# A two-layer hybrid decoder with the residual kept token-major, and 512-column matmuls throughout

## The chip, the cores and the metric

The kernel runs on one core of a Trainium2 chip. TensorE (PE) multiplies: it loads a stationary operand of 128x128 and streams a moving operand of up to 512 columns past it, and adds the products up in PSUM. VectorE (DVE) and ScalarE (ACT) do elementwise work, GpSimd (POOL) a little of it, and SyncE (SP) issues most of the loads. The metric is device time in microseconds for one execution, as the median of several runs. Lower is better.

## The reference

The input x is 256 tokens of 2048 features, in float32. Each of two layers adds a mixer and then a dense MLP to the residual, each behind an RMS norm:

```python
for i in range(DEPTH):                       # DEPTH = 2
    hn = rms_norm(h, mixer_norm[i])
    mix = diff_attention(hn, ...) if i == 0 else mamba2_mixer(hn, ...)
    h = h + mix
    h = h + jnp.square(jax.nn.relu(rms_norm(h, mlp_norm[i]) @ w1[i])) @ w2[i]
```

`diff_attention` has 8 heads. For each, two query and two key vectors of 128 are normed and rotated, two causal softmax maps are subtracted, and the result multiplies values of width 256; the heads are normed and projected by w_o. `mamba2_mixer` projects to gates z, channels x, B, C and 64 time steps dt, runs a causal convolution of 4 taps, a chunked scan over two chunks of 128 tokens, a gate and a group norm, and projects from 4096 to 2048 features by w_out. The MLP goes from 2048 to 8192 and back.

## The kernel before

Everything is held feature-major: a tile has 128 features on the partitions and the 256 tokens along the free dimension. The residual is eight tiles `h[j]` of [128, 2, 256], 256 features each.

All weights are float32 and come in pieces of [128, 1024], 512 KB, by `load` (SP's queue, six buffers `raw`). `split_weights` splits each piece exactly into two float32r parts: ACT rounds to `wh`, DVE subtracts to get `wl` (L138, L139, four buffers each). Activations are split in the same way; an entry of `acts` is [128, 2, 256], the high part beside the low part. A product is then made of three terms: high weight times high activation, high times low, and low times high.

`sub_block` multiplies one piece, 128 output features over 8 k-tiles of 128. It has two forms. Where the accumulator has room for one sum (*narrow*), each k-tile takes three matmuls of 256 columns, L151, L152 and L158, 24 for a piece. Where it has room for two (*wide*), high and low activations are streamed together, 512 columns, into two sums (L149), and L158 adds the low weights: 16 matmuls for a piece. The two sums are added afterwards on ACT and DVE.

- narrow: `pair` (queries, keys, Mamba's in-projection `win`), `block` (`wdt`), `half_pair` (the output projections `wo` and `wout`, eight k-tiles at a time, each result added to `h` by L280);
- wide: `wide_pair` (both MLP matrices; w1's sums are joined by L479 and L480, w2's added to `h` by L284);
- `token_pair` (values): activations are stationary and 256 weight columns stream (L211), 24 matmuls for a piece. The result has tokens on the partitions.

The order of the work is written out by hand. `Side` holds two queues of generators (norms, attention inside a head, convolution, scan); `side.tick()` is called three times for each piece and issues the next step of each queue between the matmuls. So the small matmuls of these steps, into PSUM tiles `aux`, lie among the projections.

The norms: `norm_input(j)` squares `h[j]` on ACT (L235), adds the squares up on POOL (L236), and makes the next stage's activations, `h[j] * gain` split in two, by L243 on ACT and L244 on DVE. `norm_stats` adds up over the partitions with a matrix of ones (L126) and computes 1/rms as a tile `rstd` that is the same on all partitions; it is multiplied in behind the projection (L481 in the MLP, L705 and L584 in Mamba). At the start x is loaded in eight tiles, between the first weights. The last stage stores `h[j]` by SP's queue as each is done.

Of the kernel before, what the change touches and what calls it, by code (L numbers as in the profile page):

```python
# [36 lines left out]
# columns of the packed parameters  # L37
# [51 lines left out]
def trunk_kernel(ctx: ExitStack, tc: tile.TileContext, x, par, rope, qk, wv, wo, w10, w20, win, wdt, wout, w11, w21, out):  # L89
# [27 lines left out]

    def split(src, t):
        """float32 [P, n] -> the two float32r parts that add up to it, t [P, 2, n]."""
        S.copy(out=t[:, 0, :], in_=src)  # L120
        V.tensor_tensor(out=t[:, 1, :], in0=src, in1=t[:, 0, :].bitcast(F32), op=ALU.subtract)

    def sums(out, t):
        """The sums over the partitions of what was split, on every partition."""
        for i in range(2):
            PE.matmul(out, lhsT=ones_r, rhs=t[:, i, :], start=(i == 0), stop=(i == 1))  # L126

    side = Side()
    h = [const.tile([P, 2, T], F32, name=f"h{j}") for j in range(KT // 2)]
    sqacc = const.tile([P, 2, T], F32, name="sqacc")  # L130

# [10 lines left out]
    def sub_block(w, acts, acc, start, stop):  # L142
        """128 output features over 8 k-tiles. acc has room for a sum [P, T], or for two [P, 2, T] that add up to it."""
        wh, wl = w
        wide = len(acc.shape) == 3
        for k, act in enumerate(acts):
            wk = wh[:, k * P:(k + 1) * P]
            if wide:
                PE.matmul(acc, lhsT=wk, rhs=act, start=(start and k == 0), stop=False)  # L149
            else:  # L150
                PE.matmul(acc, lhsT=wk, rhs=act[:, 0, :], start=(start and k == 0), stop=False)  # L151
                PE.matmul(acc, lhsT=wk, rhs=act[:, 1, :], start=False, stop=False)  # L152
            if k % 4 == 3:
                side.tick()
        if wide:
            acc = acc[:, 0, :]
        for k, act in enumerate(acts):
            PE.matmul(acc, lhsT=wl[:, k * P:(k + 1) * P], rhs=act[:, 0, :], start=False, stop=(stop and k == 7))  # L158
        side.tick()

    def load(src, s, n=1):
        """A piece of the weights, [128, 1024]."""
        raw = wp.tile([P, 1024], F32, tag="raw", bufs=6, name="raw")
        w = 1024 // n
        for i in range(n):
            nc.sync.dma_start(out=raw[:, i * w:(i + 1) * w], in_=src[s, :, i * w:(i + 1) * w])
        return raw

    def block(src, acts, acc):
        """128 output features over 16 k-tiles."""  # L170
        raw = [load(src, s) for s in range(2)]
        for s in range(2):
            sub_block(split_weights(raw[s]), acts[8 * s:8 * s + 8], acc, s == 0, s == 1)
# [4 lines left out]
    def pair(src, b, acts):  # L178
        """Two blocks."""
        pp = bank()  # L180
        for t in range(2):
            block(src[b + t], acts, pp[:, t, :])
        return pp

    def wide_pair(src, b, acts):
        """Two blocks, each as two sums."""
        pp = [bank() for _ in range(2)]
        for s in range(2):
            raw = [load(src[b + t], s) for t in range(2)]
            for t in range(2):  # L190
                sub_block(split_weights(raw[t]), acts[8 * s:8 * s + 8], pp[t], s == 0, s == 1)
        return pp

    def half_pair(src, acts):
        """Two blocks of 128 output features over 8 k-tiles."""
        pp = bank()
        raw = [load(src, t) for t in range(2)]
        for t in range(2):
            sub_block(split_weights(raw[t]), acts, pp[:, t, :], True, True)
        return pp  # L200

    def token_pair(src, acts):
        """256 output features over 16 k-tiles, tokens on the partitions."""
        pp = [bank() for _ in range(2)]
        for s in range(4):
            wh, wl = split_weights(load(src, s))
            for first, w in ((True, wh), (False, wl)):
                for k in range(4):
                    for t in range(2):
                        for i in range(2 if first else 1):  # L210
                            PE.matmul(pp[t][:, 0, :], lhsT=acts[4 * s + k][:, i, t * P:(t + 1) * P], rhs=w[:, k * T:(k + 1) * T],  # L211
                                      start=(first and s + k + i == 0), stop=(not first and s + k == 6))
                    if k == 3 or (first and k == 1):
# [7 lines left out]
    def split_pair(src):  # L221
        """float32 [P, 2, T] in SBUF -> its float32r parts."""
# [6 lines left out]
    def norm_square(j):  # L229
        """The sum of the squares of h[j]."""  # L230
        if j == 0:
            S.activation(sqacc, h[j], AF.Square)
        else:
            sq = const.tile([P, 2, T], F32, tag="nsq", bufs=1, name="nsq")
            S.activation(sq, h[j], AF.Square)  # L235
            G.tensor_tensor(out=sqacc, in0=sqacc, in1=sq, op=ALU.add)  # L236

    def norm_gain(j, gain):
        """h[j] * gain, whose 1/rms comes after the projection."""
        t, parts = act_pair()  # L240
        for i in range(2):
            g = pa[:, gain + 2 * j + i:gain + 2 * j + i + 1]
            S.activation(t[:, i, 0, :], h[j][:, i, :], AF.Identity, scale=g)  # L243
            V.scalar_tensor_tensor(out=t[:, i, 1, :], in0=h[j][:, i, :], scalar=g, in1=t[:, i, 0, :].bitcast(F32),  # L244
# [3 lines left out]
    def norm_input(j, gain):  # L248
        norm_square(j)
        return norm_gain(j, gain)  # L250

    def rsqrt(pool, t, n, tag, bufs=1):
        """t ** -0.5 by exp(-ln(t) / 2) and one Newton step."""
# [9 lines left out]
    mean = const.tile([P, T], F32, name="mean")  # L263
    rstd = const.tile([P, T], F32, name="rstd")

    def norm_stats():
        V.tensor_tensor(out=mean, in0=sqacc[:, 0, :], in1=sqacc[:, 1, :], op=ALU.add)
        parts = const.tile([P, 2, T], F32R, tag="nsq", bufs=1, name="nss")
        split(mean, parts)
        yield from wait(5)  # L270
        ss = aux()
        sums(ss[:, 0:T], parts)
        yield
        V.tensor_scalar(out=mean, in0=ss[:, 0:T], scalar1=1.0 / D, scalar2=EPS, op0=ALU.mult, op1=ALU.add)
        c = rsqrt(const, mean, T, "n")
        V.tensor_copy(out=rstd, in_=c)
        yield

    def residual(pp, j):
        V.tensor_tensor(out=h[j], in0=pp, in1=h[j], op=ALU.add)  # L280

    def residual_wide(pp, dst):
        for i in (1, 0):
            V.tensor_tensor(out=dst, in0=pp[:, i, :], in1=dst, op=ALU.add)  # L284
# [6 lines left out]
    for j in range(KT // 2):  # L291
        nc.sync.dma_start(out=h[j], in_=x[j])
        if j in (0, 3, 5):
            raw.append(load(qk[len(raw) % 2], len(raw) // 2, 1 if j else 2))
    raw.append(load(qk[1], 1))
    for s in range(2):
        for j in range(4 * s, 4 * s + 4):
            xs += norm_gain(j, C_MIX0)
            if j == 4 * s:
                w = split_weights(raw[2 * s], 1 if s else 2)  # L300
        for t in range(2):
            sub_block(w if t == 0 else split_weights(raw[2 * s + 1]), xs[8 * s:8 * s + 8], first[t][:, 0, :], s == 0, s == 1)
    for j in range(KT // 2):
        norm_square(j)

    with tc.tile_pool(name="att", bufs=1) as ap:
# [18 lines left out]
        def setup():  # L325
            yield from wait(2)
            yield from norm_stats()
            V.tensor_scalar_mul(epsm, mean, EPS)
            yield

        def setup_v():
            yield from wait(20)
            rt = aux()
            for t in range(2):
                PE.matmul(rt[:, t:t + 1], lhsT=rstd[:, t * P:(t + 1) * P], rhs=ident[:, 0:1], start=True, stop=True)
            V.tensor_copy(out=rtok, in_=rt[:, 0:2])
            yield
# [108 lines left out]
        for hd in range(NH):  # L446
            qkn = ap.tile([P, 4, T], F32, tag="qkn", bufs=2, name="qkn")
            pq = qkn[:, 0:2, :]
            if hd:
                pq = pair(qk, 4 * hd, xs)  # L450
            else:
                for t in range(2):
                    S.copy(out=pq[:, t, :], in_=first[t][:, 0, :])
# [379 lines left out]
```

## Time and profile before

| | |
|---|---|
| median of 3 runs | 2554.76 us (2554.24 to 2554.98) |
| span of the profiled execution, first to last instruction | 2551.7 us |
| the same execution's time with what lies around the span | not recorded; the median is 3.06 us above the span |
| busy: PE, PEld, DVE, ACT, POOL | 100%, 92%, 67%, 52%, 2% |
| granted TensorE clock | 1.000 |
| HBM read, written | 464.78 MB, 2.16 MB |

PE is the stream of matmuls and PEld the loads of stationary operands, which overlap it. In a row of a group, the first number behind the bar is the busy time in us (overlaps counted once), the next the mean of one instruction in ns, then the engine's idle time just before the group and what ended it. In the chain of work a row is a start, a duration and what ran; consecutive matmuls there take the time by which each moved the chain on, so it shows their pitch and not their latency. A row of stretches gives, for each engine, busy time and the number of instructions, then the granted clock, the share of the DMA engines and GB/s.

### The profile page before, as it was taken

The page shows a single profiled execution, that of the slowest core. Times are in us where ns is not written, and L with a number is a line of the kernel's source. Part 1 is how long each engine was busy: PE and PEld are TensorE (multiplying, and loading weights), DVE is VectorE, ACT ScalarE, POOL GpSimd, SP SyncE. Part 2 cuts the span into 40 slices and gives each one's busy share as a digit, 9 for nine tenths or more (in the row PEclk, how much of TensorE's full clock was granted, in tenths as well). Part 3 has the DMA queues.
Part 4 walks back from the last instruction along what each step waited for, and adds up shares of the span by engine and source line. Part 5 has one row for each costly group of instructions (what it writes and reads, how often), then busy time and mean ns, then how long its engine had stood idle before and what let it go on. Part 6 is the DMA issues. An engine that isn't in the chain of part 4 may idle for free.

```text
span 2551.7 us, 42442 instructions
## 1 busy us (share of the span) xinstructions
PE 2540.0 (100%) x17314; PEld 2347.1 (92%) x17314; DVE 1710.4 (67%) x2241; ACT 1328.4 (52%) x1860; POOL 45.0 (2%) x36
## 2 busy tenths in 40 slices
PE   8999999999999999999999999999999999999999
PEld 8999999888888888889999999999988888888888
DVE  8787777655655656677786776776765565565564
ACT  6665645534534435546666565664654453453442
POOL 1000001000000000010000000000100000000000
PEclk9999999999999999999999999999999999999999
DMA  7454555555555565556556556555555555655564
GB/s 246 155 170 150 175 169 185 188 188 189 190 189 188 187 188 189 190 182 202 185 180 196 166 184 200 161 179 176 184 189 190 190 189 185 189 189 190 190 194 137
DMA packets 130212, 469.71 MB, mean 184 GB/s; under 512 B 14592, under 2 KB 15040, under 8 KB 130016
## 3 DMA queue, kind: packets, MB, share of 16 engines
q1 hardware_dynamic: 127296, 458.28, 55.8%
q10 hardware_dynamic: 2720, 8.71, 1.1%
q8 instruction: 135, 2.21, 0.4%
q14 instruction: 61, 0.50, 0.1%
HBM read 464.78 MB, written 2.16 MB: 183 GB/s over the span
## 4 chain that ended last, share of the span: by engine, by line
PE 99%; ACT 0%; DMA 0%; DVE 0%; issue 0%; SPq 0%
PE pp L149 37%; PE pp L158 31%; PE pp L151 12%; PE pp L152 12%; PE pp L211 4%; PE aux L647 1%; PE aux L126 0%; PE aux L391 0%; PE aux L648 0%; PE aux L617 0%; PE aux L420 0%; ACT act L243 0%; DMA raw<-in_qk 0%; ACT wh L138 0%; PE aux L421 0%; PE aux L604 0%
## 5 line engine op out<-in xcount | busy, mean ns | idle before, releaser
L138 ACT CAST wh<-raw 128x1024 fp32r<-128x1024 f32 (+1 forms) x867 | 907.0, 1046 | 1062.9 <-PE pp L149 739.0
L139 DVE TENSOR_TENSOR wl<-raw,wh 128x1024 fp32r<-128x1024 f32 (+1 forms) x867 | 1060.1, 1225 | 532.4 <-ACT wh L138 525.7
L149 PE MATMUL pp<-act,wh 128*128 128x512 f32 x4096 | 1025.6, 392 | 0.0
L158 PE MATMUL pp<-act,wl 128*128 128x256 f32 x6672 | 936.2, 283 | 0.0
L158 PEld LDWEIGHTS pp<-act,wl 128*128 128x128 f32 x6672 | 891.1, 191 | 43.3 <-issue 2.7
L149 PEld LDWEIGHTS pp<-act,wh 128*128 128x128 f32 x4096 | 736.6, 189 | 131.7
L151 PE MATMUL pp<-act,wh 128*128 128x256 f32 x2576 | 640.0, 285 | 6.2 <-ACT wh L138 5.7
L152 PE MATMUL pp<-act,wh 128*128 128x256 f32 x2576 | 636.3, 284 | 2.0 <-DVE act L244 1.9
L151 PEld LDWEIGHTS pp<-act,wh 128*128 128x128 f32 x2576 | 495.2, 192 | 10.9 <-ACT wh L138 5.7
L152 PEld LDWEIGHTS pp<-act,wh 128*128 128x128 f32 x2576 | 495.5, 192 | 3.4 <-DVE act L244 2.9
L284 DVE TENSOR_TENSOR h<-pp,h 128x256 f32<-128x256 f32 x256 | 107.8, 421 | 154.9 <-PE pp L158 154.9
L236 POOL TENSOR_TENSOR sqacc<-sqacc,nsq 128x512 f32<-128x512 f32 x28 | 43.8, 1564 | 1790.1 <-ACT nsq L235 1790.1
L211 PE MATMUL pp<-wh,act 128*128 128x256 f32 x512 | 69.3, 285 | 0.0
L211 PEld LDWEIGHTS pp<-wh,act 128*128 128x128 f32 x512 | 64.5, 191 | 0.5
L280 DVE TENSOR_TENSOR h<-pp,h 128x512 f32<-128x512 f32 x48 | 33.1, 690 | 46.5 <-PE pp L158 46.4
L573 DVE SCALAR_TENSOR_TENSOR cy<-u,cwb,cy 128x256 f32<-128x256 f32 x144 | 60.2, 476 | 0.0
L480 DVE TENSOR_TENSOR relu<-pp,relu 128x256 f32<-128x256 f32 x128 | 53.3, 416 | 0.0
L244 DVE SCALAR_TENSOR_TENSOR act<-h,pa,act 128x256 fp32r<-128x256 f32 x64 | 50.9, 827 | 0.3
L479 ACT COPY relu<-pp 128x256 f32<-128x256 f32 x128 | 47.7, 372 | 0.0
L481 DVE SCALAR_TENSOR_TENSOR relu<-relu,rstd 128x512 f32<-128x512 f32 x64 | 44.3, 693 | 2.2
L632 ACT ACTIVATE m<-ab,acol 128x128 f32<-128x128 f32 x128 | 42.2, 390 | 4.5 <-PE aux L648 3.3
L225 DVE TENSOR_TENSOR act<-relu,act 128x512 fp32r<-128x512 f32 x64 | 44.3, 693 | 0.2 <-ACT act L224 0.2
(168 smaller groups left out, 988.4 us busy)
## 6 DMA issues: line engine op xcount, KB each, us to landing
raw<-in_w SPq DMA_DIRECT2D x512, 512.0 KB, 3.4
raw<-in_win SPq DMA_DIRECT2D x160, 512.0 KB, 3.5
raw<-in_wout SPq DMA_DIRECT2D x64, 512.0 KB, 3.6
raw<-in_qk SPq DMA_DIRECT2D x63, 512.0 KB, 4.1
raw<-in_wv SPq DMA_DIRECT2D x32, 512.0 KB, 3.4
raw<-in_wo SPq DMA_DIRECT2D x32, 512.0 KB, 3.4
ab<-dram_a ACTq DMA_DIRECT2D x16, 512.0 KB, 5.2
h<-in_x SPq DMA_DIRECT2D x8, 256.0 KB, 5.0
```

The source lines that it names most:

```text
L138: S.copy(out=wh[:, s], in_=raw[:, s])
L139: V.tensor_tensor(out=wl[:, s], in0=raw[:, s], in1=wh[:, s].bitcast(F32), op=ALU.subtract)
L149: PE.matmul(acc, lhsT=wk, rhs=act, start=(start and k == 0), stop=False)
L151: PE.matmul(acc, lhsT=wk, rhs=act[:, 0, :], start=(start and k == 0), stop=False)
L152: PE.matmul(acc, lhsT=wk, rhs=act[:, 1, :], start=False, stop=False)
L158: PE.matmul(acc, lhsT=wl[:, k * P:(k + 1) * P], rhs=act[:, 0, :], start=False, stop=(stop and k == 7))
L211: PE.matmul(pp[t][:, 0, :], lhsT=acts[4 * s + k][:, i, t * P:(t + 1) * P], rhs=w[:, k * T:(k + 1) * T], start=(first and s + k + i == 0), ...
L244: V.scalar_tensor_tensor(out=t[:, i, 1, :], in0=h[j][:, i, :], scalar=g, in1=t[:, i, 0, :].bitcast(F32), op0=ALU.mult, op1=ALU.subtract)
L284: V.tensor_tensor(out=dst, in0=pp[:, i, :], in1=dst, op=ALU.add)
L479: S.copy(out=r[:, t, :], in_=pp[t][:, 1, :])
L480: V.tensor_tensor(out=r[:, t, :], in0=pp[t][:, 0, :], in1=r[:, t, :], op=ALU.add)
L573: V.scalar_tensor_tensor(out=y[:, i, :], in0=u[:, i, k:k + T], scalar=cwb[:, w + k:w + k + 1], in1=y[:, i, :], op0=ALU.mult, op1=ALU.add)
```

## The change

The residual becomes one token-major tile `h` of [128, 2, 2048]: tokens on the partitions, two halves of 128 tokens.

Projections into the residual (wo, wout, both w2) and the values use a new `token_block`: 512 output features, activations stationary, and 512 weight columns streaming, into two PSUM banks, one for each half of the tokens. A piece holds two k-tiles of 512 columns and takes 12 matmuls. The values of two heads are made at once. All other projections use the wide form of `sub_block`; their two sums are joined by `add_sums`.

```diff
+    def token_block(src, j, acts):
+        pp = [bank().rearrange("p a b -> p (a b)") for _ in range(2)]
+        n = src.shape[0]
+        for s in range(n):
+            w = split_weights(load(src[s, j]))
+            for i, wi in enumerate(w):
+                for k in range(2):
+                    while len(acts) <= 2 * s + k:
+                        side.tick()
+                    act = acts[2 * s + k]
+                    m = wi[:, k * NB:(k + 1) * NB]              # NB = 512
+                    for t in range(2):
+                        tok = slice(t * P, (t + 1) * P)
+                        PE.matmul(pp[t], lhsT=act[:, 0, tok], rhs=m, ...)
+                        if i == 0:
+                            PE.matmul(pp[t], lhsT=act[:, 1, tok], rhs=m, ...)
+                    if i == 0 or k:
+                        side.tick()
+    def add_sums(dst, pp):
+        for t in range(len(pp)):
+            S.copy(out=dst[:, t, :], in_=pp[t][:, 1, :])
+            V.tensor_tensor(out=dst[:, t, :], in0=pp[t][:, 0, :], in1=dst[:, t, :], op=ALU.add)
```

The next stage still wants feature-major activations, so `norm_input` becomes a generator on the side queue. It transposes the residual on TensorE into PSUM, four 128x128 blocks at a time, and `x_parts` (the former `norm_gain`) reads from there. The squares are summed along the free dimension by ACT itself; POOL and the ones matrix drop out. Where a norm's factor is wanted on all partitions (`epsm`, Mamba's `rstd`), `rows` makes it from two diagonal matrices and two small matmuls.

```diff
+    def norm_square(j):
+        for t in range(2):
+            S.activation(junk, h[:, t, cols(j)], AF.Square, accum_out=ssq[:, t, j:j + 1])
+    def norm_input(j, gain, xs):
+        for i in range(2):
+            if i == 0:
+                yield
+            ax = aux().rearrange("p (a b) -> p a b", a=2)
+            for f in range(2):
+                for t in range(2):
+                    c = NB * j + T * i + P * f
+                    PE.transpose(ax[:, f, t * P:(t + 1) * P], h[:, t, c:c + P], ident)
+            xs += x_parts(ax, 2 * j + i, gain)
+            yield
+        norm_square(j)
```

In the MLP, 1/rms is no longer multiplied in before the square: `r2 = 1 / ms` scales w2's result, one number for each token, as it is added to `h` by one DVE instruction on 512 columns.

```diff
+                V.scalar_tensor_tensor(out=r, in0=r, scalar=0.0, in1=r, op0=ALU.max, op1=ALU.mult)
+                hid += split_pair(r)
+            for j in range(4):
+                pp = token_block(w2[8 * q:8 * q + 8], j, hid)
                 for t in range(2):
+                    V.scalar_tensor_tensor(out=h[:, t, cols(j)], in0=pp[t], scalar=r2[:, t:t + 1], in1=h[:, t, cols(j)],
+                                           op0=ALU.mult, op1=ALU.add)
+                    if q == 3:
+                        after(j, t)
```

At the start x is loaded twice: feature-major into tiles `xf` as before, and token-major into `h`, in four loads of 512 KB from ACT's queue.

```diff
+            f = xp.tile([P, 2, T], F32, name=f"xf{j}")
+            nc.sync.dma_start(out=f, in_=x[j])
...
+        for j in range(4):
+            nc.scalar.dma_start(out=h[:, :, cols(j)], in_=xt[:, :, cols(j)])
```

`wdt` is one wide block (`wide_one`), and Mamba's statistics and dt work follow it as one generator, without the drain of the side queues that stood between them. The output is stored token-major, 128x512 at a time. The layouts of wv, wo, wout and w2 in memory follow the new pieces; their size stays 512 KB.

More of the change, by code (lines that the diff above doesn't have):

```diff
@@ L88, in trunk_kernel @@
 @with_exitstack
-def trunk_kernel(ctx: ExitStack, tc: tile.TileContext, x, par, rope, qk, wv, wo, w10, w20, win, wdt, wout, w11, w21, out):
+def trunk_kernel(ctx: ExitStack, tc: tile.TileContext, x, xt, par, rope, qk, wv, wo, w10, w20, win, wdt, wout, w11, w21, out):
     nc = tc.nc
@@ L116, in aux1, with rows @@
         return ps_ax.tile([P, 512], F32, tag="aux1", bufs=1, name="aux1")
+    def rows(dst, cols, name):
+        ax = aux()
+        for t in range(2):
+            dg = const.tile([P, P], F32, tag="dg", bufs=2, name=name)
+            V.tensor_scalar_mul(dg, ident, cols[:, t:t + 1])
+            PE.matmul(ax[:, t * P:(t + 1) * P], lhsT=ones, rhs=dg, start=True, stop=True)
+        V.tensor_copy(out=dst, in_=ax[:, 0:T])
     def split(src, t):
@@ L128, in trunk_kernel, with cols @@
     side = Side()
-    h = [const.tile([P, 2, T], F32, name=f"h{j}") for j in range(KT // 2)]
-    sqacc = const.tile([P, 2, T], F32, name="sqacc")
+    h = const.tile([P, 2, D], F32, name="h")
+    ssq = const.tile([P, 2, 4], F32, name="ssq")
+    NB = 512
+    def cols(j):
+        return slice(NB * j, NB * (j + 1))
     def split_weights(raw, n=1):
@@ L140, in split_weights, with sub_block, load @@
         return wh, wl
-    def sub_block(w, acts, acc, start, stop):
+    def sub_block(w, acts, k0, acc, start, stop):
         wh, wl = w
[L145 to L152, printed above, removed]
+        for k in range(8):
+            while len(acts) <= k0 + k:
+                side.tick()
+            PE.matmul(acc, lhsT=wh[:, k * P:(k + 1) * P], rhs=acts[k0 + k], start=(start and k == 0), stop=False)
             if k % 4 == 3:
                 side.tick()
[L155 to L158, printed above, removed]
+        for k in range(8):
+            PE.matmul(acc[:, 0, :], lhsT=wl[:, k * P:(k + 1) * P], rhs=acts[k0 + k][:, 0, :], start=False, stop=(stop and k == 7))
         side.tick()
-    def load(src, s, n=1):
+    def load(src, n=1):
         raw = wp.tile([P, 1024], F32, tag="raw", bufs=6, name="raw")
@@ L165, in load @@
         for i in range(n):
-            nc.sync.dma_start(out=raw[:, i * w:(i + 1) * w], in_=src[s, :, i * w:(i + 1) * w])
+            nc.sync.dma_start(out=raw[:, i * w:(i + 1) * w], in_=src[:, i * w:(i + 1) * w])
         return raw
[L169 to L173, printed above, removed]
     def bank():
         return ps.tile([P, 2, T], F32, tag="mm", name="pp")
[L178 to L183, printed above, removed]
     def wide_pair(src, b, acts):
@@ L202, in token_pair @@
[L202 to L208, printed above, removed]
-                    for t in range(2):
[L210 to L213, printed above, removed]
+        raw = [load(src[b, s]) for s in range(2)]
@@ new lines, in wide_one @@
+        for s in range(2):
+            sub_block(split_weights(raw[s]), acts, 8 * s, pp, s == 0, s == 1)
+        return pp
+    def add_sums(dst, pp):
[13 more added lines that the diff above has]
+                    m = wi[:, k * NB:(k + 1) * NB]
+                    for t in range(2):
+                        tok = slice(t * P, (t + 1) * P)
+                        PE.matmul(pp[t], lhsT=act[:, 0, tok], rhs=m, start=(s + i + k == 0), stop=(s == n - 1 and i + k == 2))
+                        if i == 0:
+                            PE.matmul(pp[t], lhsT=act[:, 1, tok], rhs=m, start=False, stop=False)
+                    if i == 0 or k:
@@ L226, in split_pair, with x_parts @@
         return parts
[L229 to L238, printed above, removed]
+    def x_parts(src, j, gain):
         t, parts = act_pair()
@@ L261, in rsqrt, with norm_mean @@
         return c
[L263 to L277, printed above, removed]
+    ms = const.tile([P, 2], F32, name="ms")
+    def norm_mean():
+        V.tensor_reduce(out=ms, in_=ssq, axis=AX.X, op=ALU.add)
+        V.tensor_scalar(out=ms, in0=ms, scalar1=1.0 / D, scalar2=EPS, op0=ALU.mult, op1=ALU.add)
     def residual(pp, j):
[L280 to L284, printed above, removed]
+        for t in range(2):
+            V.tensor_tensor(out=h[:, t, cols(j)], in0=pp[t], in1=h[:, t, cols(j)], op=ALU.add)
     xs = []
@@ L290, in trunk_kernel @@
     raw = []
[L291 to L303, printed above, removed]
+    with tc.tile_pool(name="xin", bufs=1) as xp:
+        xf = []
+        for j in range(KT // 2):
+            f = xp.tile([P, 2, T], F32, name=f"xf{j}")
+            nc.sync.dma_start(out=f, in_=x[j])
+            xf.append(f)
+            if j in (0, 3, 5):
+                raw.append(load(qk[len(raw) % 2, len(raw) // 2], 1 if j else 2))
+        raw.append(load(qk[1, 1]))
+        for j in range(4):
+            nc.scalar.dma_start(out=h[:, :, cols(j)], in_=xt[:, :, cols(j)])
+        for s in range(2):
+            for j in range(4 * s, 4 * s + 4):
+                xs += x_parts(xf[j], j, C_MIX0)
+                if j == 4 * s:
+                    w = split_weights(raw[2 * s], 1 if s else 2)
+            for t in range(2):
+                sub_block(w if t == 0 else split_weights(raw[2 * s + 1]), xs, 8 * s, first[t], s == 0, s == 1)
+    for j in range(4):
         norm_square(j)
@@ L326, in setup @@
             yield from wait(2)
-            yield from norm_stats()
-            V.tensor_scalar_mul(epsm, mean, EPS)
+            norm_mean()
+            yield from wait(2)
+            em = ap.tile([P, 2], F32, name="em")
+            V.tensor_scalar_mul(em, ms, EPS)
+            rows(epsm, em, "dge")
+            yield
+            V.tensor_copy(out=rtok, in_=rsqrt(const, ms, 2, "n"))
             yield
@@ L332, in setup_v @@
             yield from wait(20)
[L333 to L337, printed above, removed]
             lp = ap.tile([P, 2], F32, name="lp")
@@ L583, in gate @@
             g = sp.tile([P, 2, T], F32, tag="gz", bufs=2, name="gz")
-            V.tensor_tensor(out=z, in0=pp, in1=bc(rstdh, 2), op=ALU.mult)
+            add_sums(z, pp)
+            V.tensor_tensor(out=z, in0=z, in1=bc(rstdh, 2), op=ALU.mult)
             S.activation(g, z, AF.Tanh)
@@ L691, in trunk_kernel, with stats @@
         ys = {}
-        pp = bank()
-        side.add(norm_stats())
-        block(wdt[0], xs, pp[:, 0, :])
-        side.drain()
-        side.add(dt_work(pp), slow=True)
+        pdt = sp.tile([P, 1, T], F32, name="pdt")
+        add_sums(pdt, [wide_one(wdt, 0, xs)])
+        def stats():
+            norm_mean()
+            c = rsqrt(const, ms, 2, "n")
+            yield from wait(2)
+            rows(rstd, c, "dgr")
+            yield
+            yield from dt_work(pdt)
+        side.add(stats(), slow=True)
         xs_next = []
@@ L719, in out_part @@
             acts = ys[2 * q] + ys[2 * q + 1]
-            for j in range(KT // 2):
-                residual(half_pair(wout[8 * q + j], acts), j)
+            for j in range(4):
+                residual(token_block(wout[4 * q:4 * q + 4], j, acts), j)
                 if last:
-                    xs_next.extend(norm_input(j, C_MLP1))
+                    side.add(norm_input(j, C_MLP1, xs_next))
         for g in (0, 1, 2):
@@ L780 @@
     x = np.ascontiguousarray(a["x"].reshape(T, 8, 2, P).transpose(1, 3, 2, 0))
+    xt = np.ascontiguousarray(a["x"].reshape(2, P, D).transpose(1, 0, 2))
     order, conv = [], []
```

114 lines of the change are left out of this document (47 added, 67 removed).

## Prediction

> **What bounds the kernel now.** I read the page's busy shares and its chain of work first, then the waits of TensorE, then the groups with shapes kept apart, then pieces of the chain in order of time.
>
> ```profile
> span 2551.7 us, 42442 instructions
> PE 2540.0 (100%) x17314; PEld 2347.1 (92%) x17314; DVE 1710.4 (67%) x2241; ACT 1328.4 (52%) x1860; POOL 45.0 (2%) x36
> PE 99%; ACT 0%; DMA 0%; DVE 0%; issue 0%; SPq 0%
> ```
>
> TensorE is busy all the time and carries 99% of the chain. A modelled end can make an engine look busy that is not, so the waits decide:
>
> ```profile
> PE pp L151 <- ACT wh L138: 5.7, 1, 5.7
> PE pp L152 <- DVE act L244: 1.9, 2, 1.0
> PE pp L151 <- ACT act L243: 0.6, 1, 0.6
> ```
>
> These three are all of TensorE's waits: 8.2 us, nearly all in the first 20 us. So the time is the sum of what TensorE issues, and I price instructions by the pitch at which they follow each other, not by their recorded mean.
>
> ```profile
> L149 PE MATMUL pp<-act,wh 128*128 128x512 f32 x4096 | 1025.6, 392 | 0.0
> L158 PE MATMUL pp<-act,wl 128*128 128x256 f32 x6672 | 936.2, 283 | 0.0
> L151 PE MATMUL pp<-act,wh 128*128 128x256 f32 x2576 | 640.0, 285 | 6.2 <-ACT wh L138 5.7 <-ACT act L243 0.6
> L211 PE MATMUL pp<-wh,act 128*128 128x256 f32 x512 | 69.3, 285 | 0.0
> ```
>
> The counts give the work in pieces of 128x1024 weights. L149 issues 8 per piece: 512 wide pieces (both MLPs). L151 issues 8 per piece: 322 narrow ones. The values are 32 more. The means overlap (392 and 283 ns are latencies), so the pitch is taken from the chain. A wide piece in an MLP (ten pieces from the first to the last row), a narrow one in the Mamba layer, and the value projection:
>
> ```profile
> 699.91 1.84 PE pp L149 x8
> ...
> 727.84 1.84 PE pp L149 x8
> ```
> ```profile
> 1302.24 0.96 PE pp L158 x8
> ...
> 1305.12 0.96 PE pp L158 x8
> ```
> ```profile
> 35.41 3.84 PE pp L211 x32
> 39.24 0.46 PE aux L126 x2
> ```
>
> Wide: 27.93/10 = 2.793 us per piece, of which 1.84/8 = 230 ns per 512-column matmul. Narrow: 1305.12 - 1302.24 = 2.88 us, 24 matmuls at 120 ns. Values: 3.84/32 = 120 ns, again 24 per piece, 2.88 us. L126 shows another 512-column matmul at 0.46/2 = 230 ns.
>
> **The change part by part.** All three forms stream the same 6144 columns per piece. They differ in the number of matmuls: 24 narrow, 16 wide, and 12 in the new token form (2 k-tiles x 2 token halves x 3, all of 512 columns).
>
> (a) Queries and keys (64 pieces), Mamba's in-projection (160) and wdt (2) go from narrow to wide: 226 x (2.88 - 2.793) = 19.7 us less. Both prices are measured here.
>
> (b) Values (32), wo (32) and wout (64) go to the token form. Activations stationary with 512 moving columns has no row. The two 512-column rows (L149 with weights, L126 with ones stationary) agree on 230 ns, and L211 shows that which operand is stationary makes no difference at 256 columns. So I take 12 x 0.230 = 2.76 us, and 128 x 0.12 = 15.4 us less. Ends: 240 ns (two 256-column matmuls, 2.88 us), and the slope between the rows: (230 - 119.4)/256 = 0.432 ns per column, 221 ns for 512, 2.65 us; 119.4 is (2.793 - 1.84)/8.
>
> (c) Both w2 (256 pieces) go from wide to token: 256 x 0.033 = 8.4 us less.
>
> (d) Added on TensorE: `norm_input` transposes the new residual in three places, 4 column blocks x 8 = 96 transposes of 128x128 float32. The same form exists as L617:
>
> ```profile
> L617 PE MATMUL aux<-ident,xss 128*128 128x128 f32 x64 | 9.6, 272 | 0.0
> ```
> ```profile
> 1194.00 0.95 PE pp L158 x8
> ...
> 1195.91 0.44 PE aux L617 x4
> ...
> 1197.30 0.96 PE pp L158 x8
> ```
>
> From L158 to L158 with four transposes between them it is 3.30 us, against 2.88 without: 0.42, near the 0.44 of the row. 24 x 0.44 = 10.6 us more, all on the path. (The Trainium skill, "TensorE: Matmul & The Clock Gate", Part 4, gives about 275 ns per 128x128 transpose in a kernel's context and says that transposes do not count as activity for the clock. By it 96 would cost an estimated 26.4 us and halve the gain. The trace agrees with its 272 ns as latency, not as pitch.)
>
> (e) The norm's sums over partitions go (8 matmuls), four small ones each go and come:
>
> ```profile
> L126 PE MATMUL aux<-nss,ones_r 128*128 128x256 f32 x8 | 2.2, 332 | 0.0
> ```
>
> At 0.12 each that is 1 us less. The additions on POOL (2% busy) go too; TensorE never waited for them.
>
> (f) Start. ACT's queue issues four loads of the token-major x, 2.1 MB, beside SP's.
>
> ```profile
> 6.00:9.00 3.00, 2.41 (x9) 1.82 (x9) 2.90 (x7) 2.63 (x7) 0.00 (x0) 1.00 1.03 382
> 12.00:15.00 3.00, 3.00 (x20) 3.00 (x20) 3.00 (x4) 3.00 (x7) 1.29 (x1) 1.00 1.05 414
> ```
> ```profile
> 16.70 1.91 DVE act L244 x2
> ```
>
> The DMA is full (share over 1, about 0.41 MB per us), so x and the first weights are delayed by up to 2.1/0.41 = 5.1 us. But the four narrow pieces here were paced by ACT and DVE preparing activations (L244 ends the chain's wait at 18.6), which covers most of it, and the four issues in front of ACT's first activation cost it little, since it waits for the parameters then. DVE also loses its slow company: L244 took 0.9 us there while POOL added squares. Bounds -0.5 and +5.1; I take +1.5, nearer to the covered end.
>
> (g) End. Two 128x512 results become ready together, instead of two 128x256 at the last:
>
> ```profile
> 2547.25 0.96 PE pp L158 x8
> 2548.24 0.44 DVE h L284
> 2548.70 0.42 DVE h L284
> ```
> ```profile
> L280 DVE TENSOR_TENSOR h<-pp,h 128x512 f32<-128x512 f32 x48 | 33.1, 690 | 46.5 <-PE pp L158 46.4
> ```
> ```profile
> out<-h SPq DMA_DIRECT2D x7, 256.0 KB, 4.1
> out<-h SPq DMA_DIRECT2D x2, 128.0 KB, 1.7
> ```
>
> Two additions of 0.69 (L280) less the 0.23 by which the first is ready early: 1.15 against 0.86; and a 256 KB store, 1.7 to 4.1 us. Bounds 0 and +2.7; I take +0.6, as no loads compete there.
>
> (h) Layer ends. The next stage's k-tiles 12 to 15 now wait for residual (2 x 0.69), transposes, ACT and DVE. Before an MLP, two pieces (5.6 us) cover it. wdt has only one piece of cover, and TensorE waited there already:
>
> ```profile
> 1137.10 1.51 DVE act L244
> ...
> 1138.65 0.39 PE pp L152
> ```
>
> ```profile
> L243 ACT ACTIVATE act<-h,pa x64: 491/494/508, 3.7 to 1834.5; 128x256 fp32r<-128x256 f32 x64
> L244 DVE SCALAR_TENSOR_TENSOR act<-h,pa,act x64: 470/476/1551, 5.4 to 1836.3; 128x256 fp32r<-128x256 f32 x64
> ```
> ```profile
> L139 DVE TENSOR_TENSOR wl<-raw,wh 128x1024 fp32r<-128x1024 f32 (+1 forms) x867 | 1060.1, 1225 | 532.4 <-ACT wh L138 525.7
> ```
>
> That L244 took 1.51 us (minimum, median and maximum: 470/476/1551 ns), beside POOL again, and TensorE lost 1.0 us. Afterwards POOL is silent, but transposes follow the last residual. They are issued behind the first 8 and the first 16 matmuls of the stage, so the second four end at 2.79 + 2 x 0.43 = 3.65 us; two L243 and one L244 make the last activation ready at 3.65 + 0.98 + 0.48 = 5.1, or 6.3 with a weight split (L139, 1.22) queued between. It is wanted at 3.65 + 7 x 0.23 = 5.3. Bounds -1 and +2; I take +0.5.
>
> (i) Moved to ACT and DVE: 56 narrow pairs now need `add_sums`, two L479 and two L480 each. Hidden so far as DVE has room:
>
> ```profile
> L480 DVE TENSOR_TENSOR relu<-pp,relu 128x256 f32<-128x256 f32 x128 | 53.3, 416 | 0.0
> L479 ACT COPY relu<-pp 128x256 f32<-128x256 f32 x128 | 47.7, 372 | 0.0
> L284 DVE TENSOR_TENSOR h<-pp,h 128x256 f32<-128x256 f32 x256 | 107.8, 421 | 154.9 <-PE pp L158 154.9
> ```
> ```profile
> 1132.00:1833.00 701.00, 700.02 (x5816) 684.89 (x5815) 525.54 (x730) 420.36 (x657) 10.72 (x7) 1.00 0.57 182
> 1700.00:1720.00 20.00, 20.00 (x169) 20.00 (x169) 18.32 (x32) 18.96 (x35) 0.00 (x0) 1.00 0.43 136
> ```
>
> In the Mamba layer DVE goes from 525.5 to 525.5 + 40 x 0.83 = 559 of some 690 us, 81%. The fullest 20 us go from 18.3 to about 19.8. Four buffers of split weights stand between DVE and TensorE, so I cost it at 0; without that cover it is 0.83 us per pair. In w2 DVE gains: 64 scaled additions of about 0.69 replace 256 L284, 64 us less. The loads keep their size (512 KB) and their number.
>
> Sum: -19.7 - 15.4 - 8.4 + 10.6 - 1.0 + 1.5 + 0.6 + 0.5 = -31.3. The profiled span of 2551.7 becomes 2520.4. The median of the runs is 3.06 us above that span (launch and end lie around it), and I leave this as it is: 2554.76 - 31.3 = 2523.5 us.
>
> **The rivals.** (1) *The token form's pitch is 240 ns* (the moving side costs the same per column however wide): its 384 pieces cost 0.12 us more than I say, +46.1 us, 2569.6 us, slower than before. It decides from 31.3/(384 x 12) = 6.8 ns per matmul, a pitch of 236.8. For it: 256 columns at 120 with either operand stationary. Against it: both 512-column rows.
> (2) *DVE comes late in the Mamba layer and in attention.* If none of `add_sums` is covered, 56 x 0.83 = +46.5 us: 2570. If only the fullest stretches fail, about a quarter, 2535. For it: 92% in the fullest stretch. Against it: no wait of TensorE for DVE after 24 us save the one at wdt.
> (3) *The token form is faster than its rows*: what a 512-column matmul costs beyond the slope is the change of the stationary operand, and it vanishes when the activations are loaded: 2.65 us per piece, 384 x 0.11 = 42 us less: 2481. For it: only the intercept of 9 ns. Against it: L126 keeps the same stationary and still shows 230. The Trainium skill, the same page, "Back-to-back issue gap", says N/2.4 + 2.5 ns, 215.8 at 512 columns; the rows here are 14 ns above it.
> (4) *The start pays in full*: +3.6, 2527. This is in the range.
>
> **How the numbers follow.** My case has a chance of 0.76 with a range of its own from 2512 (the small terms at their low ends, the token pitch 2 ns lower) to 2534 (start, end and wdt at their upper ends: +7.2 and some 3 us of late DVE). Rival 1 has 0.04, rival 2 mild 0.09 and full 0.04, rival 3 0.04; 0.03 is for costs that I did not see and that eat the gain. The range 2510 to 2540 holds the first case and the mild rival 2, about 0.85. A measurement of this kernel can tell about 0.2% (5 us) from no change. Faster: 0.76 + 0.09 + 0.04, 0.89; same 0.03; slower 0.08.
>
> **What the profile after would show.** Right: TensorE still at 100% with almost no waits; no narrow pieces; 482 x 8 wide matmuls at 230 ns; 384 x 12 token matmuls, twelve of them in 2.76 us in the chain; 96 transposes in groups of four at 0.44; POOL nearly silent. Wrong: twelve token matmuls in 2.88 or 2.65; waits of TensorE for DVE `wl` or for copied sums in the Mamba layer; a first stretch more than 5 us longer; a gap at each layer end.

## The result, and the profile after

The changed kernel takes 2512.21 us (median of 4 runs, 2510.96 to 2512.81); the kernel before took 2554.84 beside it (2554.24 to 2554.98). The ratio is 0.9833, with a 95% interval of 0.9819 to 0.9847: 42.6 us faster. The profiled spans differ by 42.5 us (2551.7 and 2509.2). I had forecast 31.3. A span lies some 1.75 us under the time of its own execution (2510.96 and 2509.2 here). So the 3.06 us that I put down to launch and end were these 1.75, and 1.3 by which the profiled execution of the kernel before was faster than the median; the 31.3 do not depend on it.

The page of the changed kernel, its busy shares and its chain by engine, and then all of TensorE's waits:

```profile
span 2509.2 us, 33804 instructions
PE 2493.1 (99%) x13038; PEld 2122.0 (85%) x13038; DVE 1668.7 (67%) x2158; ACT 1310.0 (52%) x1919; POOL 1.2 (0%) x8
PE 99%; DMA 1%; SPq 0%; issue 0%; DVE 0%; ACT 0%; DVEq 0%
```
```profile
PE pp L162 <- DVE act L241: 11.8, 3, 11.1
```

TensorE is still the whole chain, with 4276 matmuls fewer. Its only waits are three for the first activations, 11.8 us in the first 21 us. POOL is silent. None of TensorE's waits names the copied sums or `wl`. So the answer to "where did the time go" is again a sum over pitches. The groups, shapes kept apart:

```profile
L162 PE MATMUL pp<-act,wh 128*128 128x512 f32 x3856 | 979.3, 394 | 11.8 <-DVE act L241 11.8
L216 PE MATMUL pp<-wh,act 128*128 128x512 f32 x1536 | 601.3, 391 | 0.0
L218 PE MATMUL pp<-wh,act 128*128 128x512 f32 x1536 | 599.0, 390 | 0.0
L166 PE MATMUL pp<-act,wl 128*128 128x256 f32 x3856 | 540.8, 283 | 0.0
L216 PE MATMUL pp<-wl,act 128*128 128x512 f32 x1536 | 413.4, 391 | 0.0
L259 PE MATMUL aux<-ident,h 128*128 128x128 f32 x96 | 14.4, 272 | 0.0
```

There are 3856 = 482 x 8 wide matmuls, the narrow form is gone, and 3 x 1536 = 384 x 12 are token matmuls. Their mean durations (390 to 394 ns) say nothing about which 512-column form is dearer. The chain does: a wide piece, and then four token pieces in a w2:

```profile
432.75 1.84 PE pp L162 x8
435.54 1.84 PE pp L162 x8
```
```profile
702.53 1.13 PE pp L216 x5
...
705.25 1.13 PE pp L216 x5
707.97 1.13 PE pp L216 x5
710.69 1.13 PE pp L216 x5
```

The wide piece is 435.54 - 432.75 = 2.79 us, as before. The token piece is 2.72, not the 2.76 that I had put in: 2.72/12 = 226.7 ns per matmul. Among the small matmuls of attention the same five token matmuls took longer:

```profile
114.42 1.21 PE pp L216 x5
...
123.52 1.15 PE pp L216 x5
...
127.60 1.16 PE pp L216 x5
```

That is 230 to 242 ns each. So 512 columns have no single price, and this is what the forecast missed.

The start, in order of time; then ACT's issues (shortest, median, longest in ns) and the median landing times of the loads:

```profile
1.77 7.83 ACTq L301 DMA_DIRECT2D h<-in_xt  x4
9.65 0.91 ACT L240 ACTIVATE act<-xf,pa 128x256 fp32r<-128x256 f32 x2 [6.63 <-DMA xf<-in_x]
11.12 1.22 PE L162 MATMUL pp<-act,wh 128*128 128x512 f32 x2 [11.12 <-DVE act L241]
12.84 2.93 PE L162 MATMUL pp<-act,wh 128*128 128x512 f32 x6 [0.50 <-DVE act L241]
16.65 2.00 PE L162 MATMUL pp<-act,wh 128*128 128x512 f32 x8
```
```profile
L301 ACTq DMA_DIRECT2D h<-in_xt x4: 547/560/662, 1.8 to 9.1; - x4
xf<-in_x SPq DMA_DIRECT2D x8, 256.0 KB, 6.6
h<-in_xt ACTq DMA_DIRECT2D x4, 512.0 KB, 9.4
out<-h SPq DMA_DIRECT2D x8, 256.0 KB, 2.5
```

ACT's four issues are spread over 7.83 us, and its first activation, behind them in ACT's program, began at 9.65; before it was 3.66. The issues themselves took 2.3 us together. Between them ACT waited: in the trace each of the later three waits for an earlier load to land, and they began at 3.76, 4.80 and 9.06, 0.02 us after the landings (3.74, 4.78, and 9.04 for the first of the four). What the first activation needs, the first tile of x and the parameters, had landed by 3.74. The fifth piece begins at 26.18, before at 23.48.

The first matmuls come at half pace: six of 512 columns in 2.93 us, later eight in 2.00. By their starts they are 427 ns apart up to 15.57, and before, 256-column ones are 213 ns apart from 8.53 to 13.65. The trace's record of the granted clock begins only at 15.84 and 13.94, so a row of an earlier stretch says 1.00 for lack of a record. From the first matmul to full pace it is 4.7 us in this trace, 8.3 before and 4.9 to 7.9 in the experiments. A matmul at half pace takes twice its time, so an execution can lose up to (8.3 - 4.7)/2 = 1.8 us against another by this alone (an estimate); spans and medians below can differ by as much.

At the other end, the last addition and store:

```profile
2503.97 0.69 PE pp L216 x3
2504.69 0.75 DVE h L490
```

From the end of the matmul that releases the first of these additions it is 4.55 us to the end, against 3.47 before. The last token matmul (0.23) still runs beside it.

### The profile page after: what moved, and what is told of

Read it like the earlier page. It is cut to its first block, busy times and chain, and to the rows that moved or that the text cites. A ratio compares the mean times of both kernels' runs of the same rounds, so it can differ in the third digit from the quotient of the medians.

```text
span 2509.2 us, 33804 instructions
## 1 busy us (share of the span) xinstructions
PE 2493.1 (99%) x13038; PEld 2122.0 (85%) x13038; DVE 1668.7 (67%) x2158; ACT 1310.0 (52%) x1919; POOL 1.2 (0%) x8
## 4 chain that ended last, share of the span: by engine, by line
PE 99%; DMA 1%; SPq 0%; issue 0%; DVE 0%; ACT 0%; DVEq 0%
PE pp L162 35%; PE pp L216 28%; PE pp L166 18%; PE pp L218 14%; PE aux L650 1%; PE aux L135 0%; PE aux L397 0%; PE aux L259 0%; DMA raw<-in_qk 0%; PE aux L620 0%; PE aux L651 0%; PE aux L426 0%; DMA xf<-in_x 0%; PE aux L427 0%; PE aux L607 0%; PE aux L420 0%
## 5 line engine op out<-in xcount | busy, mean ns | idle before, releaser
L162 PE MATMUL pp<-act,wh 128*128 128x512 f32 x3856 | 979.3, 394 | 11.8 <-DVE act L241 11.8
L162 PEld LDWEIGHTS pp<-act,wh 128*128 128x128 f32 x3856 | 693.0, 189 | 138.1 <-ACT wh L152 11.1
L216 PE MATMUL pp<-wh,act 128*128 128x512 f32 x1536 | 601.3, 391 | 0.0
L218 PE MATMUL pp<-wh,act 128*128 128x512 f32 x1536 | 599.0, 390 | 0.0
L166 PEld LDWEIGHTS pp<-act,wl 128*128 128x128 f32 x3856 | 524.6, 191 | 37.7 <-issue 1.7
L166 PE MATMUL pp<-act,wl 128*128 128x256 f32 x3856 | 540.8, 283 | 0.0
L216 PE MATMUL pp<-wl,act 128*128 128x512 f32 x1536 | 413.4, 391 | 0.0
L216 PEld LDWEIGHTS pp<-wh,act 128*128 128x128 f32 x1536 | 288.5, 188 | 60.2 <-issue 1.0
L218 PEld LDWEIGHTS pp<-wh,act 128*128 128x128 f32 x1536 | 288.8, 188 | 58.1
L216 PEld LDWEIGHTS pp<-wl,act 128*128 128x128 f32 x1536 | 286.6, 188 | 59.9 <-issue 1.0
L490 DVE SCALAR_TENSOR_TENSOR h<-pp,r,h 128x512 f32<-128x512 f32 x64 | 45.1, 747 | 43.0 <-PE pp L216 43.0
L485 DVE SCALAR_TENSOR_TENSOR relu<-relu 128x512 f32<-128x512 f32 x64 | 44.3, 692 | 2.2
L284 DVE TENSOR_TENSOR h<-pp,h 128x512 f32<-128x512 f32 x48 | 31.0, 685 | 19.7 <-PE pp L216 19.7
```

The source lines that it names most:

```text
L162: PE.matmul(acc, lhsT=wh[:, k * P:(k + 1) * P], rhs=acts[k0 + k], start=(start and k == 0), stop=False)
L166: PE.matmul(acc[:, 0, :], lhsT=wl[:, k * P:(k + 1) * P], rhs=acts[k0 + k][:, 0, :], start=False, stop=(stop and k == 7))
L216: PE.matmul(pp[t], lhsT=act[:, 0, tok], rhs=m, start=(s + i + k == 0), stop=(s == n - 1 and i + k == 2))
L218: PE.matmul(pp[t], lhsT=act[:, 1, tok], rhs=m, start=False, stop=False)
L485: V.scalar_tensor_tensor(out=r, in0=r, scalar=0.0, in1=r, op0=ALU.max, op1=ALU.mult)
L490: V.scalar_tensor_tensor(out=h[:, t, cols(j)], in0=pp[t], scalar=r2[:, t:t + 1], in1=h[:, t, cols(j)], op0=ALU.mult, op1=ALU.add)
```

## The experiments

All times are medians beside the changed kernel's 2512.21 (span 2509.2). In the runs of the kernel before that were made beside them it took 2554.1 to 2555.0.

**1. The narrow form back in queries, keys, in-projection and wdt** (tests term (a)).

```diff
+            if wide or (start and k == 0):
                 PE.matmul(acc, lhsT=wk, rhs=acts[k0 + k], ...)
+            else:
+                PE.matmul(acc[:, 0, :], lhsT=wk, rhs=acts[k0 + k][:, 0, :], ...)
+                PE.matmul(acc[:, 1, :], lhsT=wk, rhs=acts[k0 + k][:, 1, :], ...)
```

> The changed kernel with the 226 pieces of queries, keys, win and wdt back at three 256-column matmuls for each k-tile (high and low activations still go into two sums, so the copies and additions on ACT and DVE stay; only the first k-tile of each bank keeps its 512-column matmul, which opens both sums). Theory A (the gain of this part is TensorE's pitch alone: 2.88 against 2.79 us a piece): 226 x 0.087 = +19.7 us against the changed kernel, span about 2529. Rival (the gain came from somewhere else, the two sums cost time on ACT and DVE): clearly less than +10, or more than +30 if ACT and DVE were close to being late.

Measured: 2528.51 (2528.16 to 2529.05), ratio to before 0.9899 (0.9883 to 0.9916), span 2526.4. That is 16.3 us more by median and 17.2 by span. The edit leaves the first k-tile of each bank wide, so 1695 of 1808 k-tiles went back, the work of 212 pieces: 0.077 to 0.081 us for each in place of 0.087. The term holds, a little smaller.

**2. Token matmuls of both w2 as two of 256 columns** (tests the pitch of the token form, and rival 1).

```diff
+                            for u in range(n_parts):
+                                c = slice(NB // n_parts * u, NB // n_parts * (u + 1))
+                                PE.matmul(pp[t][:, c], lhsT=act[:, lo, tok], rhs=m[:, c], ...)
```

> The changed kernel with each 512-column matmul of the 256 pieces of w2 made as two of 256 columns (the very first of each bank stays whole). Theory A (a matmul costs its columns at 2.4 GHz plus 13.3 ns, 120 ns at 256 and 226.7 at 512): 24 x 0.120 = 2.88 against 2.72 us a piece, 256 x 0.16 = +41 us, span about 2550. Rival 1 of the prediction (same cost per column, whatever the width): 0. Prediction's own price (119.4 and 230 ns): 256 x (2.866 - 2.76) = +27 us.

Measured: 2552.07, ratio 0.9989 (0.998 to 0.9998), span 2550.1: 40.9 more by span, 39.9 by median. Of 3072 matmuls of 512 columns 3008 became two of 256 (the first of each bank stays whole), so one costs 39.9/3008 = 13.3 ns less than two of 256, 13.6 by span. With 120 ns for one of 256 that is 240 - 13.3 = 226.7, the pitch of the chain. Rival 1 said 0 and falls; 230 would have made 30 (3008 x 10 ns), and falls as well.

**3. High and low weights in turn, 512 and 256 columns alternating** (is it each change of width that costs?).

```diff
             PE.matmul(acc, lhsT=wh[:, k * P:(k + 1) * P], rhs=acts[k0 + k], ...)
-        for k in range(8):
             PE.matmul(acc[:, 0, :], lhsT=wl[:, k * P:(k + 1) * P], rhs=acts[k0 + k][:, 0, :], ...)
```

> The changed kernel with the two kinds of matmul in a wide piece (512 columns with the high weights, 256 with the low ones) in turn, k-tile by k-tile, in place of eight and then eight. Theory A (each change from 256 to 512 columns and back costs some 20 ns, which is why the wide 512-column matmul reads 230 ns and the token one 227): 8 changes there and back for each piece in place of 1, 482 x 7 x 0.02 = +67 us, span about 2577. Theory B (230 ns is the price of a 512-column matmul that streams activations, whatever stands before it): 0, span 2509.

Measured: 2526.04 (ratio 0.9888, 0.9874 to 0.9903), 13.8 us more by median and 14.5 by span: between the theories, and neither is right. The chain in the first w1 quarter of an MLP, then in the second (17 k-tiles between the first and the last row of each), and one group of waits:

```profile
440.03 0.23 PE pp L162
...
445.92 0.23 PE pp L162
```
```profile
599.78 0.23 PE pp L162
...
605.79 0.23 PE pp L162
```
```profile
PE pp L163 <- DVE wl L153: 5.9, 7, 1.1
```

A k-tile of 512 and 256 columns took 5.89/17 = 0.3465 us in the first and 6.01/17 = 0.3535 in the second; in runs of eight it is 2.793/8 = 0.349. So a change of width has no fixed price of its own: 16 changes in a piece save 0.02 us in one stretch and cost 0.035 in the other. By matmul starts the third and fourth quarters of this MLP come at 0.353 too. Why the first is faster stays open. 5.9 us of the loss are another thing: the low weights are wanted 8 matmuls earlier, and DVE is late.

**4. Half as many changes of width: runs of 16 high, 8 low, 16 high, 24 low for each pair of wide blocks** (is it what follows a run of 256-column matmuls?).

```diff
+            if s == 0:
+                high(w[0], ...); high(w[1], ...); low(w[1], ...); low(w[0], ...)
+            else:
+                low(w[0], ...); high(w[0], ...); high(w[1], ...); low(w[1], ...)
```

> The changed kernel with the order in a pair of wide blocks high, high, low, low, low, high, high, low, so that it changes between 512 and 256 columns 4 times for four pieces instead of 8. Theory A (20 ns for a change there and back): 2 x 0.02 = 0.04 us less for each of 120 pairs, -4.8 us, span about 2504.5, and the mean pitch in the wide pieces falls from 230.5 towards 228.5. Theory B (the price goes by shape and operand, not by order): 0.

Measured: 2507.76 (2506.96 to 2508.57), ratio 0.9817 (0.9803 to 0.9832): 4.45 less by median, 2.9 by span (its profiled execution needed 7.9 us from the first matmul to full pace, the changed kernel's 4.7). The chain:

```profile
440.17 3.65 PE pp L184 x16
443.82 0.95 PE pp L192 x8
444.78 3.65 PE pp L184 x16
448.43 2.87 PE pp L192 x24
```

Sixteen wide matmuls take 3.65 us, 228 ns each; eight take 1.84, 230. By their starts in the changed kernel, the first five 512-column matmuls behind a run of eight 256-column ones come 229 to 235 ns apart, the following ones 226 to 227. The first two of 256 behind 512 come a little early (114 and 119 ns), so a whole piece loses some 20 ns: 2.793 against 8 x (226.7 + 120) = 2.773.

**5. Transposes twice** (tests term (d)).

```diff
-                    PE.transpose(ax[:, f, t * P:(t + 1) * P], h[:, t, c:c + P], ident)
+                    for _ in range(2):
+                        PE.transpose(ax[:, f, t * P:(t + 1) * P], h[:, t, c:c + P], ident)
```

> Every one of the 96 TensorE transposes of residual tiles is issued twice into the same PSUM place. Theory A (the rows: 0.44 us for four in TensorE's order, all of it on the path): 24 times 0.44, 10.6 us more than the changed kernel, some 2522.8. Theory B (275 ns for each, the skill's figure, all on the path): 26.4 more, some 2538.6. Theory C (transposes lie in TensorE's waits and cost nothing): 0 more, 2512.2.

Measured: 2522.47 (2522.19 to 2523.3), ratio 0.9877 (0.986 to 0.9893): 10.3 more by median, 11.2 by span. Its trace has 192 transposes, each still recorded with 272 ns:

```profile
L260 PE MATMUL aux<-ident,h 128*128 128x128 f32 x192 | 24.9, 272 | 0.0
```

So four more cost 0.43 to 0.47 us, 107 to 117 ns each. In the changed kernel's trace the four start 108 to 110 ns apart; the next matmul starts 28 ns behind the fourth, but then takes some 86 ns longer than usual: 0.44 in all. The Trainium skill ("TensorE: Matmul & The Clock Gate", Part 4) gives about 275 ns; the 272 ns are a latency and not what a transpose costs in a full stream.

**6. One more 128x256 addition on DVE for each joined sum outside the MLPs** (tests term (i) and rival 2). Its result is not used.

```diff
+            for _ in range(more):
+                V.tensor_tensor(out=dve_junk, in0=dst[:, t, :], in1=dst[:, t, :], op=ALU.add)
```

> One further 128x256 add on DVE, some 0.42 us, stands behind each add that joins two PSUM sums outside the MLPs (the added result is not used): about 112 of them, some 47 us of DVE's time in the q, k and SSM stages. Theory A (DVE's new adds lie beside TensorE's matmuls with room to spare): under 3 us more than the changed kernel's 2512.2. Theory B (DVE's part is late, as in the prediction's second rival, and was hidden only just): 15 to 47 more, 2527 to 2559, with waits of TensorE on DVE's adds or parts in the chain of waits.

Measured: 2513.22 (2512.92 to 2514.02), ratio 0.984 (0.9825 to 0.9855): 1.0 more. The Mamba layer in the changed kernel and then here (the third engine is DVE):

```profile
1119.00:1798.00 679.00, 679.00 (x3776) 574.28 (x3775) 543.35 (x809) 440.12 (x745) 0.00 (x0) 1.00 0.57 188
```
```profile
1122.00:1802.00 680.00, 680.00 (x3777) 574.06 (x3776) 572.49 (x891) 439.29 (x744) 0.00 (x0) 1.00 0.54 188
```

DVE works 29 us more there, 84% of the time, and the kernel hardly moves. The joined sums are covered with room.

**7. The token-major input on SP's queue** (tests term (f)).

```diff
-            nc.scalar.dma_start(out=h[:, :, cols(j)], in_=xt[:, :, cols(j)])
+            nc.sync.dma_start(out=h[:, :, cols(j)], in_=xt[:, :, cols(j)])
```

> The four 512 KB loads of the token-major input are issued by SP, behind its first weight loads, in place of ACT. Theory A (the start): in the changed kernel ACT's four issues take 7.83 us while the DMA queues are full, ACT's first activation begins at 9.65 in place of 3.66, and the first matmul at 11.12 in place of 5.65; with ACT free, the first four pieces end near 23.5 to 24 again in place of 26.35: 2 to 3 us less than the changed kernel's 2512.2, some 2509.5. Theory B (the 2 MB themselves are the cost: the DMA engines are full to 27 us whichever queue issues them): 0 to 1 us less, since the input or the second weights then land later by as much.

Measured: 2511.98 (2511.97 to 2512.14), ratio 0.9835 (0.982 to 0.985): nothing, theory B's number. But the trace does not show theory B. The first matmul is at 5.50 again, and what it wins is lost later; TensorE's waits and two stretches (the number before the last two is the granted clock):

```profile
PE pp L162 <- DVE act L241: 6.5, 2, 5.5
PE aux L135 <- ACT sqr L129: 2.7, 1, 2.7
```
```profile
24.00:26.00 2.00, 1.96 (x3) 0.95 (x4) 1.13 (x2) 2.00 (x6) 0.00 (x0) 0.50 1.01 404
28.00:30.00 2.00, 2.00 (x8) 1.71 (x8) 1.97 (x7) 2.00 (x3) 0.00 (x0) 0.50 0.79 281
```

In the compiled order the sums of a head's norm (L135) stood ahead of the fifth piece, and ACT had the first norm's squares (L248) queued in front of what L135 needs. TensorE waited 2.7 us, and then ran at half its clock for 6.8 us.

**8. The late input: SP's queue, behind two more weight loads, and the squares in the side work of the next pair.**

```diff
         def setup():
+            for j in range(4):
+                nc.sync.dma_start(out=h[:, :, cols(j)], in_=xt[:, :, cols(j)])
+                yield
             yield from wait(2)
+            for j in range(4):
+                norm_square(j)
+                yield
             norm_mean()
```

> As the run with the token-major input on SP's queue, but the four loads stand behind two more weight loads and the squares of the first norm are computed in the side work of the next pair of blocks, so that nothing of them stands on ACT ahead of the weight parts of the fifth piece. Theory A (what the earlier queue won was lost again in a 2.7 us wait of TensorE and at half the granted clock behind it, 24 to 30 us): no wait over 1 us there, the granted clock at 1.0, and the 2 to 3 us of the start come back: some 2509 in place of the changed kernel's 2512.2. Theory B (2 MB more in the first 30 us cost the same wherever they stand): 2511.5 to 2512.5, with a wait on weights or squares elsewhere in the first 60 us.

Measured: 2507.55 (2507.05 to 2510.09), ratio 0.9819 (0.9806 to 0.9833): 4.7 less by median, 3.9 by span, more than the 2 to 3 expected. The first token matmul starts at 34.30; in the changed kernel it starts at 38.31, and in experiment 7 at 39.30. Its waits:

```profile
PE pp L162 <- ACT wh L152: 5.7, 1, 5.7
PE aux L124 <- DVE dge L123: 2.0, 1, 2.0
PE pp L162 <- DVE act L241: 0.9, 1, 0.9
```

I had expected no wait over 1 us there; one of 2.0 is left, without loss of the clock in this trace. (One of the five executions took 2510.09 at a mean granted clock of 0.999, the others 2507.05 to 2507.89 at 1.000; whether it lost the clock at this wait is not recorded.) So some 4 us of the start were for the place of the loads and the squares, not for the bytes.

**9. The two gains together**, with the input as in experiment 7, and as in experiment 8:

> The loads of the token-major input on SP's queue, and the order of 16 high, 8 low, 16 high, 24 low matmuls for each pair of wide blocks outside nothing but the interleaved ones, as in the run with half the changes of width. Theory A (the two gains are in different stages and add): 4.5 from the order and 2 to 3 from the start, some 2505. Theory B (the input's queue gives nothing): 2507.8, as the order alone.

> The same late input loads and squares together with the order of 16 high, 8 low, 16 high, 24 low matmuls for a pair of wide blocks. Theory A: the order's 4.5 us and the start's 2 to 3 add to the changed kernel's 2512.2: some 2505. Theory B (no gain from the start): 2507.8.

Measured: 2506.80 (2506.08 to 2508.3), ratio 0.9815 (0.9801 to 0.983), and 2503.87 (2503.26 to 2504.89), ratio 0.9803 (0.9789 to 0.9816). The first lies between its two theories, 1 us under the order alone. The second is the fastest version of all, 50.6 us under the 2554.47 of before beside it. It lacks 0.8 us of the full sum of both gains (2512.21 - 4.45 - 4.66 = 2503.10). It has a 2.02 us wait at the place of experiment 8's 2.00, but here the clock fell:

```profile
28.00:32.00 4.00, 3.47 (x15) 3.47 (x16) 3.96 (x9) 3.83 (x8) 0.00 (x0) 0.57 0.80 286
```

## Why the prediction was right, and where a step was off

The direction, the bound (TensorE's own stream) and the mechanism were right, and the time lies in the range, near its low end; it is also at the very end of the range that I gave to my own case, 2512 to 2534. (The terms named for that end come to 2510.2, 2523.5 less 4.1 and less 4608 x 0.002, and not to 2512.) By the starts of successive matmuls in both traces, stage by stage (a matmul's price is the distance to the next start, and the 86 ns of the matmul behind four transposes are booked under (d)):

| term | forecast, us | measured, us |
|---|---|---|
| (a) narrow to wide, 226 pieces | -19.7 | -18.4 |
| (b) wv, wo, wout to token, 128 pieces | -15.4 | -18.0 |
| (c) w2 to token, 256 pieces | -8.4 | -18.5 |
| (d), (e) transposes, norm sums | +9.6 | +9.55 |
| (f) start | +1.5 | +3.05 |
| (g) end | +0.6 | +0.85 |
| (h) wdt | +0.5 | -1.0 |
| (i) sums on ACT and DVE | 0 | 0 |
| everything else | 0 | -0.1 |
| sum | -31.3 | -42.5 |

The step that failed is the price of the token form, the 230 ns on which the two 512-column rows agree. Both rows had come right behind other work: L149 behind a run of eight 256-column matmuls in every piece, L126 as two alone. Neither was a steady run. In w2, where next to nothing breaks the stream, the pitch is 226.7, and (c) was 10 us too small. In (b) the small matmuls of attention and of the Mamba layer break the runs, the mean pitch is 230 to 233, and 230 was nearly right there; (b) came out larger because its 128 pieces had cost 372.6 us before, 2.91 each, and not the 2.88 of the rows I took. The same breaks make (a) smaller than forecast: wide 512-column matmuls come at 232 to 234 in those stages and at 230 in the MLPs. Outside (c) the misses nearly cancel, from +1.6 to -2.6 and -1.1 in all; that part is luck.

- Rival 1 (240 ns) is refuted by experiment 2. Rival 3 had the sign right: there was something beyond the slope, and part of it vanished, but not with the activations loaded as stationary operand; it vanishes in long runs of 512 columns. It gave 10 of the 42 us. The 215.8 ns that follow from the formula in the Trainium skill ("TensorE: Matmul & The Clock Gate", "Back-to-back issue gap"), there for a single matmul in isolation, are not reached: the steady pitch is 10.9 ns above it.
- Rival 2 is refuted by experiment 6, with 29 us more of DVE's time in the stage where it was feared.
- (f) had its size inside its bounds (the fifth piece is 2.70 late, and the first four should have been 0.35 shorter, which stands under (a)), but "the four issues in front of ACT's first activation cost it little" was wrong: behind issues that wait for landings, ACT began 6 us later than before. Experiments 7 and 8 show that the start was worth 4 us, and that freeing ACT alone gives none of it. Nor were the first four pieces before paced by ACT and DVE alone: from 8.53 to 13.65 their matmuls come back to back, at half pace.
- (d) is confirmed by experiment 5 and by the starts: 8.5 us up to the next matmul and 24 x 0.086 = 2.1 in that matmul, 10.55 against the 10.6 forecast.
- (h) came out at its lower bound: the wait before wdt went, since the compiled order puts a run of wide matmuls behind the second four transposes, and no wait follows:

```profile
1120.69 0.44 PE aux L259 x4
...
1122.07 0.44 PE aux L259 x4
1122.51 3.45 PE pp L162 x14
```

## What to carry to other kernels

Where TensorE is the whole chain, price a matmul by the distance between starts, and take it from a run as long and as unbroken as the one it is to go into; a row that stands behind other widths is too dear for a steady stream. A load issued by a computing engine stands in that engine's program, and if the issue waits for an earlier load to land, as ACT's fourth did until 9.06 us here, all behind it waits too; so put what is not wanted soon behind what is, and move the work that depends on it too. An earlier start counts only if what comes next is early as well: follow the chain to the first stage without waits before booking the gain.

## What the runs showed of the hardware that was not expected

- Steady float32r matmuls with a new stationary operand each time: 120 ns for 256 columns and 226.7 for 512, so (226.7 - 120)/256 = 0.417 ns per column and 13.3 ns besides. Experiment 2 gives the same 13.3 ns by medians.
- Behind a run of eight 256-column matmuls, the first five of 512 take up to 8 ns longer; with 512 and 256 in turn there was 0.3465 us per k-tile in one stretch and 0.3535 in another, in the same kernel. The cause stays open.
- The granted clock fell to 0.50 behind a wait of 2.72 us (experiment 7 and the first version of experiment 9) and one of 2.02 (experiment 9, second version), not behind one of 2.00 (experiment 8). All stretches of the clock's record up to the kernel's last matmul are multiples of 3.41 us: 10.24 at full and 6.83 at half clock in experiment 7, 13.65 and 3.41, and 17.07 and 3.41, in experiment 9. In the 3.41 us that end with a fall, TensorE had stood idle for 2.2, 1.86 and 1.96 us; in the piece of experiment 8's record, divided in the same way, that holds most of its wait it was 1.80. These idle times are estimates, since the profile models the ends of matmuls, and so few cases give no threshold. The Trainium skill ("TensorE: Matmul & The Clock Gate", Part 1) puts the return to half clock after at least one idle window of about 3.4 us and says that the window runs freely. The waits here were shorter than that, and the measurement decides; that two nearly equal ones ended differently fits a free-running window.
- The issues of 512 KB loads from ACT took 0.55 to 0.66 us each even with the DMA full. The 7.83 us of the four, and the 2.96 us of two of SP's (0.33 each, the second at 8.59 behind a landing at 8.57), are rows merged over waits for landings.
